# Host-side layouts for a streaming HGRN2 / forgetting-attention layer: inputs by feature, cached forget bias added on VectorE

## The chip, the cores and the metric

The kernel runs on one NeuronCore of one Trainium2 chip. The metric is device time in microseconds (us), the median of several runs; data that the host rearranges before the launch or after it is not in the time. TensorE (PE) multiplies and transposes, ScalarE (ACT) and VectorE (DVE) evict and compute elementwise, GpSimd (POOL) does small elementwise work and issues some DMAs, and SyncE (SP) issues the rest. 16 DMA engines move the data.

## The reference, cut to what matters

Two request groups go through one layer with the same weights: a prompt of 2048 tokens and 8 running streams of 16 tokens (the sample, 128 rows together). One projection feeds three mixers; forgetting attention of the sample reads 4096 cached rows of every stream:

```python
hq, hf, hi, hgate, fq, fk, fv, fgate, fflog, mq, mgate = _split_in(x @ w_in)
logf = jax.nn.log_sigmoid(fflog + b_forget)
# sample: keys, values, log forget values = cache followed by the new rows
D = jnp.cumsum(jnp.concatenate([past_logf, logf], axis=1), axis=1)
s = jnp.einsum('bthd,bshd->bhts', q, k) * (FX_DIM ** -0.5)
s = s + Dq[..., :, None] - Dk[..., None, :]      # the forget bias of a cached row is -Dk, up to a constant
p = jax.nn.softmax(jnp.where(mask, s, -jnp.inf), axis=-1)
o_fx = p @ v
o_mem = cross attention of mq into 256 memory rows (cached ones for the sample)
o_hg = gated linear recurrence of hq, hf, hi
y = layernorm(DN_ALPHA * x + concat(gated o_hg, o_fx, o_mem) @ w_out)
```

Besides y the outputs are the keys, values and log forget values of the new rows, the memory keys and values, and the recurrence states. All arrays are float32. x has 1024 features, w_in 3844 columns; the four forgetting heads have 64 features each.

## The kernel before, in words

TensorE contracts over the partitions, so both operands of a projection must have the features on the partitions. Tokens arrive with tokens on the partitions. `load_xT` (L248) loads half a tile (128 tokens x 512 features, buffer `xr`, three of them), lets TensorE transpose it in four pieces into a PSUM bank `tr`, and splits it into a rounded part (`xh`, ACT) and a rest (`xl`, DVE). Every projection is then three products per 128 features, 24 matmuls in all; the text calls these 24 matmuls one project. `load_w` and `split_next` (L275, L287) do the same split with the weights, 256 columns (a chunk) at a time.

Two passes go over 14 chunks of columns. Pass 1 has prompt tiles 0 to 7 and the sample tile in three groups of 384 tokens, pass 2 has tiles 8 to 15 (groups of 384, 384 and 256 tokens). An "f" chunk takes two projects per group, each with up to 384 columns moving; a "t" chunk (fox values, HGRN values) takes one project per tile with 256 or 260 columns moving. Pass 1 is 93 projects and pass 2 is 90. Results are evicted by ACT and DVE and spilled to DRAM from buffers that are double. `ev_fk` (L369) also transposes the new keys back to token rows for the output `p_fox_k`, as `mem_keys` (L481) does for the memory keys.

Other streams are woven between the matmuls of the projects. `tick` (L1103) is called four times per project, advances a clock by 0.25 and lets each stream take as many steps as an interpolation table (`PROG`, L1098) asks for. The first stream is the sample's: attention into the cached memory (4 pairs of streams), then forgetting attention over the caches (4 pairs), then its recurrence. It takes `DECODE_STEPS + 9` steps between clock 28 and clock 159; the row maxima of the prompt's forgetting attention run between 112 and 161. Steps only fix the traced order; a planner then orders the instructions of each engine by this priority and by simulated readiness.

`decode` (L619) handles one pair of streams. First the scores: for each of 8 chunks of 512 cached rows (1 for the memory) and each of the two streams it fetches a key tile (`kv`, 128 rows on partitions, 4 x 256 elements, 512 KB), transposes its eight 128x128 blocks on TensorE in two groups of four, ACT copies each group to a buffer `kT`, and each of these four copies is a step. As the fifth step it computes the scores in PSUM (`ds`, one bank): a matmul of the forget bias rows against a 0/1 matrix (`indr` x `rb`; the bias is held as a rounded part and a rest, 16 rows), then 4 x 2 matmuls of `kT` against the queries on quarters of the array; DVE takes the row maximum (L645) and ACT copies the scores to `S` (L646). After a softmax step come the values: two steps per chunk, four transposes of `S`, a DVE copy, and 32 small matmuls against two value tiles (`dv`). Key and value tiles share a ring of three buffers (`B_KV`), fetched one ahead on the SP queue; `rb` has two buffers and is fetched on the POOL queue.

After the passes, from about 975 us, come the prompt's mixers and the output projection, which work on spilled data.

Of the kernel before, what the change touches and what calls it, by code (L numbers as in the profile page):

```python
# [20 lines left out]
B_KV, B_KT, B_PJ, B_TR, B_DS = [3, 4, 3, 2, 1]  # L21
# [10 lines left out]

_CONST_PARTS = [
    ("ident", 128), ("lm", 192), ("bm", 128), ("ones", 128),
    ("tri", 128), ("cst", 128), ("cts", 128), ("sufblk", 128), ("nmask", 224), ("ind", 128), ("ind4", 128),
# [11 lines left out]
def _constants():  # L47
# [29 lines left out]
    r = np.arange(16)  # L77
    rowbh = (p // 64) * 4 + (p // 16) % 4
    put("ind", (r[:, None] % 8) == rowbh[None])
# [8 lines left out]
def kernel(  # L88
# [4 lines left out]
    w_mem_kv, w_out, ln_g, ln_b, consts,  # L93
# [8 lines left out]
    mem = mem_prompt[0]  # L102
    st_in = state_hgrn[0]
    ck = cache_fox_k[0].rearrange("b s h d -> b s (h d)")
    cv = cache_fox_v[0].rearrange("b s h d -> b s (h d)")
    clf = cache_fox_logf[0]
    cmk = cache_mem_k[0].rearrange("b s h d -> b s (h d)")
    cmv = cache_mem_v[0].rearrange("b s h d -> b s (h d)")
    win = w_in[0]
    wkv = w_mem_kv[0]  # L110
# [3 lines left out]
    o_pk = p_fox_k[0, 0].rearrange("t h d -> t (h d)")  # L114
    o_pv = p_fox_v[0, 0].rearrange("t h d -> t (h d)")
    o_pl = p_fox_logf[0, 0]
    o_mk = p_mem_k[0, 0].rearrange("t h d -> t (h d)")
    o_mv = p_mem_v[0, 0].rearrange("t h d -> t (h d)")
    o_sk = s_fox_k[0].rearrange("b t h d -> (b t) (h d)")
# [27 lines left out]
    s_r = dr.tile([4, 2, 8, 4096], F32, name="s_r")  # L147
# [17 lines left out]
    indr = ca.tile([16, 128], F32R, name="indr")  # L165
# [10 lines left out]
    def setup():  # L176
# [6 lines left out]
        DVE.tensor_copy(indr, const("ind")[0:16])  # L183
# [50 lines left out]
    # ------------------------------------------------------------------ input projections  # L234
# [13 lines left out]
    def load_xT(hi, lo, off, src):  # L248
        for half in range(2):
            xr = sg.tile([128, 512], F32, name="xr", bufs=B_XR)  # L250
            SP.dma_start(xr, src[:, half * 512 : half * 512 + 512])
            pt = ptr()
            for j in range(4):
                PE.transpose(pt[:, j, :], xr[:, j * 128 : j * 128 + 128], ident)
            d = slice(half * 4, half * 4 + 4)
            ACT.copy(hi[:, d, off : off + 128], pt)
            DVE.tensor_tensor(out=lo[:, d, off : off + 128], in0=pt, in1=hi[:, d, off : off + 128].bitcast(F32),
                              op=ALU.subtract)
# [4 lines left out]
    def fetch_ahead():  # L263
        while at["fetched"] < min(len(jobs), at["split"] + B_WR):
            job = jobs[at["fetched"]]
            job["raw"] = wp.tile([128, KW, 260], F32, name="wraw", bufs=B_WR)
            o, k = 0, job["k"]
            for s in job["srcs"]:
                n = s.shape[1]
                SP.dma_start(job["raw"][:, :, o : o + n],  # L270
                             s[128 * k : 128 * (k + KW)].rearrange("(k p) c -> p k c", p=128))
                o += n
            at["fetched"] += 1
# [13 lines left out]
    def load_w(srcs, w, pool=None):  # L287
        hi = (pool or wp).tile([128, 8, 260], F32R, name="whi")
        lo = (pool or wp).tile([128, 8, 260], F32R, name="wlo")
        for k in range(0, 8, KW):  # L290
            jobs.append(dict(srcs=srcs, w=w, hi=hi, lo=lo, k=k))
# [77 lines left out]
    def ev_fk(ps, mt, g):  # L369
# [13 lines left out]
        npt = g["np"] // 128  # L383
        SP.dma_start(o_pk[g["p0"] : g["p0"] + g["np"], c].rearrange("(j p) c -> p j c", p=128), kt[:, 0:npt, :])
        if g["s"]:
            SP.dma_start(o_sk[:, c], kt[:, npt, :])
            POOL.tensor_copy(ksT[:, mt, :], kf[:, n - 128 : n])
# [29 lines left out]
    def wc(a, n=256):  # L417
        return [win[:, a : a + n]]

    CHUNKS = [  # L420
        ("t", [win[:, 2560:2816], win[:, 3072:3076]], 260, ev_fv),
# [15 lines left out]
    def load_group(xg, gi, tiles, first=None):  # L437
# [3 lines left out]
        for j, t in enumerate(tiles):  # L441
            load_xT(hi, lo, j * 128, xs if t == "s" else xp[t * 128 : t * 128 + 128])
# [31 lines left out]
    # memory keys and values of the prompt group, and the forget bias of the cached rows  # L474
# [6 lines left out]
    def mem_keys(wk):  # L481
        for mt in range(2):
            ps = feature_major(wk, mt, mh, ml, 256)
            ACT.copy(mkT[:, mt, :], ps)
            pt = ptr()
            for j in range(2):
                PE.transpose(pt[:, j, :], mkT[:, mt, j * 128 : j * 128 + 128], ident)
            kt = ev("r", 256, bufs=1).rearrange("p (j c) -> p j c", c=128)
            ACT.copy(kt, pt[:, 0:2, :])
            SP.dma_start(o_mk[:, mt * 128 : mt * 128 + 128].rearrange("(j p) c -> p j c", p=128), kt)  # L490
# [22 lines left out]
    def cache_bias():  # L513
# [5 lines left out]
        a = oth[:, 0:256, :]  # L519
        POOL.tensor_tensor(out=a, in0=cur[:, 1:257, :], in1=off.unsqueeze(1).to_broadcast([128, 256, 4]), op=ALU.add)  # L520
        rh = mpool.tile([128, 4, 256], F32R, name="cbh")
        rl = mpool.tile([128, 4, 256], F32R, name="cbl")
        av = a.rearrange("p i h -> p h i")
        pin(ACT.copy(rh, av))
        DVE.tensor_tensor(out=rl, in0=av, in1=rh.bitcast(F32), op=ALU.subtract)
        for i, t in enumerate((rh, rl)):
            for bb in range(8):
                r0 = 4 * (bb % 2)
                SP.dma_start(s_r[bb // 2, i, r0 : r0 + 4].rearrange("h (k i) -> k h i", i=256),
                             t[16 * bb : 16 * bb + 16].bitcast(F32))  # L530
# [6 lines left out]
    def after1(i):  # L537
        if i == 0:
            for j in range(2):
                load_xT(mh, ml, j * 128, mem[j * 128 : j * 128 + 128])  # L540
            cache_scan()
        elif i == 1:
            mem_w.append(load_w([wkv[:, 0:256]], 256, pool=mpool))
        elif i == 2:
            split_next(mem_w[0][2])
            mem_keys(mem_w[0])
            mem_w.append(load_w([wkv[:, 256:512]], 256, pool=mpool))
# [5 lines left out]
    # ------------------------------------------------------------------ sample attention over the caches  # L553
# [36 lines left out]
    def cache_tile(src, r0, n):  # L590
        def f():
            t = dpool.tile([128, 4, 256], F32, name="kv", tag="kv", bufs=B_KV)
            SP.dma_start(t[:, 0 : n // 128, :], src[r0 : r0 + n].rearrange("(j p) c -> p j c", p=128))
# [11 lines left out]
    for kc, vc, rows, n in ((cmk, cmv, 256, 256), (ck, cv, 4096, 512)):  # L605
        for p in range(4):
            for src in (kc, vc):
                for c in range(0, rows, n):
                    for bb in range(2):
                        cache_issues.append(cache_tile(src[2 * p + bb], c, n))  # L610
# [8 lines left out]
    def decode(p, qbd, ns, new, dst, s_gate):  # L619
        nch = ns * 128 // 512 if new else 1  # L620
        cw = 512 if new else 256
        st = cw // 128
# [3 lines left out]
        for c in range(nch):  # L626
            kt = []
            for bb in range(2):
                kr = next_cache()
                for hp in range(2):  # L630
                    pt = ptr()
# [704 lines left out]
```

## Time and profile before

| what | value |
|---|---|
| median of 3 runs | 1681.04 us (1679.24 to 1684.19) |
| profiled execution, span from first to last instruction | 1683.6 us |
| PE busy | 1606.2 us, 95% |
| DVE, ACT, POOL busy | 47%, 35%, 11% |
| DMA, share of the 16 engines; bytes moved | 53%; 248.10 MB |
| mean granted TensorE clock | 0.989 |

The profiled execution's own time is its span, 1683.6 us, which lies inside the spread of the three runs. "Busy" for PE joins overlapping matmuls, and their ends are modelled, so the cost of an inserted instruction is best read from the start times of the matmuls around it.

### The profile page before, as it was taken

The page shows a single profiled execution, that of the slowest core. Times are in us where ns is not written, and L with a number is a line of the kernel's source. Part 1 is how long each engine was busy: PE and PEld are TensorE (multiplying, and loading weights), DVE is VectorE, ACT ScalarE, POOL GpSimd, SP SyncE. Part 2 cuts the span into 40 slices and gives each one's busy share as a digit, 9 for nine tenths or more (in the row PEclk, how much of TensorE's full clock was granted, in tenths as well). Part 3 has the DMA queues.
Part 4 walks back from the last instruction along what each step waited for, and adds up shares of the span by engine and source line. Part 5 has one row for each costly group of instructions (what it writes and reads, how often), then busy time and mean ns, then how long its engine had stood idle before and what let it go on. Part 6 is the DMA issues. An engine that isn't in the chain of part 4 may idle for free.

```text
span 1683.6 us, 31554 instructions
## 1 busy us (share of the span) xinstructions
PE 1606.2 (95%) x12885; PEld 1268.0 (75%) x12885; DVE 793.2 (47%) x1600; ACT 586.0 (35%) x1279; POOL 184.7 (11%) x251
## 2 busy tenths in 40 slices
PE   7999999999999998999999999989999999999998
PEld 7999998888887787788777886746566565567776
DVE  4222222221233234455446523267757666667785
ACT  4323333323342433023321033355434333343341
POOL 0610000000000220001001022321010110100000
PEclk9999999999999999999999999999999999999999
DMA  7555464466467764766556477596444343322321
GB/s 233 180 137 157 123 183 144 145 200 188 147 180 246 197 187 120 230 166 169 157 150 195 116 168 140 121 215 182 112 98 110 89 101 95 105 85 63 108 95 57
DMA packets 273984, 248.10 MB, mean 147 GB/s; under 512 B 44846, under 2 KB 251630, under 8 KB 273840
## 3 DMA queue, kind: packets, MB, share of 16 engines
q1 hardware_dynamic: 219408, 209.52, 41.4%
q0 software_dynamic: 54432, 36.56, 11.0%
q8 instruction: 102, 1.67, 0.4%
q14 instruction: 42, 0.34, 0.1%
HBM read 192.28 MB, written 53.64 MB: 146 GB/s over the span
## 4 chain that ended last, share of the span: by engine, by line
PE 74%; DMA 16%; DVE 4%; ACT 2%; issue 1%; SPq 1%; POOL 0%; DVEq 0%; ACTq 0%
PE pj L132 34%; PE o L132 10%; PE h L132 6%; PE pv L132 5%; PE f L132 5%; DMA kv<-in_cache_fox_v_dram 4%; PE tr L633 3%; PE ds L132 3%; DMA wraw<-in_w_in_dram 3%; PE dv L132 2%; DMA fP<-s_fg 2%; DMA hF<-s_f 2%; DMA xr<-in_x_prompt_dram 2%; PE tr L132 1%; PE L L132 1%
## 5 line engine op out<-in xcount | busy, mean ns | idle before, releaser
L132 PE MATMUL pj<-xh,whi 128*128 128x384 f32 (+1 forms) x1056 | 366.2, 347 | 6.1 <-DVE fmx L960 4.8
L132 PE MATMUL pj<-xl,whi 128*128 128x384 f32 (+1 forms) x1056 | 349.5, 331 | 0.0
L132 PE MATMUL pj<-xh,wlo 128*128 128x384 f32 (+1 forms) x1056 | 349.3, 331 | 0.0
L132 PEld LDWEIGHTS pj<-xh,whi 128*128 128x128 f32 x1056 | 200.9, 190 | 27.1 <-issue 16.7
L132 PEld LDWEIGHTS pj<-xl,whi 128*128 128x128 f32 x1056 | 200.8, 190 | 7.7 <-issue 3.7
L132 PEld LDWEIGHTS pj<-xh,wlo 128*128 128x128 f32 x1056 | 199.8, 189 | 2.0 <-issue 1.8
L960 DVE TENSOR_REDUCE fmx<-pj 128x1 f32<-128x512 f32 (+3 forms) x160 | 96.9, 609 | 84.7 <-PE pj L132 83.7
L1046 ACT ACTIVATE fP<-f 128x512 f32<-128x512 f32 (+3 forms) x144 | 73.1, 527 | 150.1 <-PE f L132 142.4
L635 ACT COPY kT<-tr 128x512 f32<-128x512 f32 (+1 forms) x144 | 81.0, 563 | 125.5 <-PE tr L633 125.0
L132 PE MATMUL pj<-whi,xh 128*128 128x256 f32 (+1 forms) x408 | 121.3, 298 | 0.0
L281 DVE TENSOR_TENSOR wlo<-wraw,whi 128x1024 fp32r<-128x1024 f32 (+1 forms) x60 | 76.4, 1273 | 95.3 <-ACT whi L280 94.7
L326 ACT ACTIVATE e<-pj 128x384 f32<-128x384 f32 (+1 forms) x96 | 45.4, 474 | 207.2 <-PE pj L132 196.9
L132 PE MATMUL pj<-wlo,xh 128*128 128x256 f32 (+1 forms) x408 | 117.5, 288 | 0.0
L1019 DVE TENSOR_TENSOR facc<-facc,fP 128x512 f32<-128x512 f32 (+3 forms) x144 | 83.8, 597 | 71.3 <-ACT fP L1046 71.0
L132 PE MATMUL pj<-whi,xl 128*128 128x256 f32 (+1 forms) x408 | 117.0, 287 | 0.0
L132 PE MATMUL pv<-fP,fV 128*64 128x512 f32 (+3 forms) x288 | 103.5, 551 | 4.2 <-ACT fP L1046 3.9
L132 PE MATMUL f<-fq,fk 68*128 68x512 f32 (+5 forms) x320 | 100.7, 406 | 1.9 <-DMA fk<-s_kk 0.9
L132 PEld LDWEIGHTS f<-fq,fk 68*128 68x128 f32 (+1 forms) x320 | 54.1, 193 | 55.3 <-issue 45.9
L132 PEld LDWEIGHTS pj<-whi,xh 128*128 128x128 f32 x408 | 78.0, 191 | 10.0 <-issue 9.1
L633 PE MATMUL tr<-cb,kv 128*128 128x128 f32 x544 | 83.5, 274 | 1.4 <-DMA kv<-in_cache_fox_k_dram 1.2
L280 ACT CAST whi<-wraw 128x1024 fp32r<-128x1024 f32 (+1 forms) x60 | 62.8, 1047 | 60.3 <-DMA wraw<-in_w_in_dram 55.6
L1032 POOL DMA_DIRECT2D fk<-s_kk x40 | 40.0, 999 | 399.9 <-PE f L132 399.9
(328 smaller groups left out, 2786.7 us busy)
## 6 DMA issues: line engine op xcount, KB each, us to landing
kv<-in_cache_fox_k_dram SPq DMA_DIRECT2D x64, 512.0 KB, 5.0
kv<-in_cache_fox_v_dram SPq DMA_DIRECT2D x64, 512.0 KB, 4.9
wraw<-in_w_in_dram SPq DMA_DIRECT2D x56, 512.0 KB, 5.4
fk<-s_kk POOLq DMA_DIRECT2D x40, 256.0 KB, 4.8
xr<-in_x_prompt_dram SPq DMA_DIRECT2D x32, 256.0 KB, 4.1
y<-in_x_prompt_dram SPq DMA_DIRECT2D x16, 512.0 KB, 3.3
out_dram<-y SPq DMA_DIRECT2D x16, 512.0 KB, 2.6
fk1m<-s_kk POOLq DMA_DIRECT2D x20, 272.0 KB, 7.8
```

The lines of the kernel that those rows point to most:

```text
L132: PE.matmul(out, lhsT=lhsT, rhs=rhs, start=start, stop=stop)
L280: pin(ACT.copy(hi[:, r, :w], raw[:, :, :w]))
L281: pin(DVE.tensor_tensor(out=lo[:, r, :w], in0=raw[:, :, :w], in1=hi[:, r, :w].bitcast(F32), op=ALU.subtract))
L326: ACT.activation(e, ps, AF.Sigmoid)
L633: PE.transpose(pt[:, j, :], kr[:, j, hp * 128 : hp * 128 + 128], ident)
L635: ACT.copy(k2[:, 0:cw], pt[:, 0:st, :].rearrange("p j c -> p (j c)"))
L960: DVE.tensor_reduce(out=mx[:, hh, tt, c : c + 1], in_=ps, axis=AX.X, op=ALU.max)
L1019: DVE.tensor_tensor(out=acc[hh][:, t0:], in0=acc[hh][:, t0:], in1=PT[hh][:, t0:], op=ALU.add)
L1032: POOL.dma_start(k1, s_kk[64:132, hs, cs])
L1046: ACT.activation(pT[:, t0:], ps[:, t0:], AF.Exp)
```

## The change

The host now writes the inputs into DRAM in the order in which tiles read them, and turns outputs back afterwards.

- x and the prompt's memory tokens lie by feature; `load_xT` loads [128 features, 4, 128 tokens] and splits it at once, with no transpose.
- weights lie so that each partition reads one contiguous row; a fetch is one DMA.
- cached keys lie as [stream, 2, 128 features, rows]; a key tile is read as [128, 2, 512] and goes straight into the score matmuls. The transposes, the ACT copies and the `kT` buffers are gone; the ring `B_KV` has five buffers, fetched three ahead. Cached values lie so that each partition reads one contiguous row of 4 KB.
- the forget bias is kept in float32 (not as two rounded rows), 8 rows per pair of streams; it is fetched on the SP queue as a [128, 512] tile, each row repeated 16 times, and one DVE instruction adds it to the scores, writes `S` and takes the maximum. The bias matmul, and for the forgetting attention the ACT copy to `S`, are gone.
- new keys and memory keys are written by feature, without transposes; the 16 small stores of the log forget values are one; states are read and written by partition.
- a score chunk is one step, not five: `DECODE_STEPS` goes from 277 to 133, inside the same table `PROG`.

```diff
-B_KV, B_KT, B_PJ, B_TR, B_DS = [3, 4, 3, 2, 1]
+B_KV, B_PJ, B_TR, B_DS = [5, 3, 2, 1]
...
     def load_xT(hi, lo, off, src):
         for half in range(2):
-            xr = sg.tile([128, 512], F32, name="xr", bufs=B_XR)
-            SP.dma_start(xr, src[:, half * 512 : half * 512 + 512])
-            pt = ptr()
-            for j in range(4):
-                PE.transpose(pt[:, j, :], xr[:, j * 128 : j * 128 + 128], ident)
             d = slice(half * 4, half * 4 + 4)
-            ACT.copy(hi[:, d, off : off + 128], pt)
+            xr = sg.tile([128, 4, 128], F32, name="xr", bufs=B_XR)
+            SP.dma_start(xr, src[:, d, :])
+            ACT.copy(hi[:, d, off : off + 128], xr)
...
-        pt = ptr()
-        nt = n // 128
-        for j in range(nt):
-            PE.transpose(pt[:, j, :], kf[:, j * 128 : j * 128 + 128], ident)
-        kt = ev("r", n, bufs=1).rearrange("p (j c) -> p j c", c=128)
-        ACT.copy(kt, pt[:, 0:nt, :])
...
+        SP.dma_start(p_fox_k[c, g["p0"] : g["p0"] + g["np"]], kf[:, 0 : g["np"]])
...
+    def key_tile(src, b, r0, n):
+        def f():
+            t = dpool.tile([128, 2, 512], F32, name="kv", tag="kv", bufs=B_KV)
+            SP.dma_start(t[:, :, 0:n], src[b, :, :, r0 : r0 + n].rearrange("c p s -> p c s"))
+            return t
...
     def bias_tile(p, c):
         def f():
-            t = dpool.tile([16, 512], F32R, name="rb", bufs=2)
-            POOL.dma_start(t, s_r[p].rearrange("i r s -> (i r) s")[:, c * 512 : c * 512 + 512])
+            t = dpool.tile([128, 512], F32, name="rb", bufs=2)
+            SP.dma_start(t, s_r[p, :, c * 512 : c * 512 + 512].unsqueeze(1).to_broadcast([8, 16, 512]))
...
         for c in range(nch):
-            kt = []
-            for bb in range(2):
-                kr = next_cache()
-                for hp in range(2):
-                    pt = ptr()
-                    for j in range(st):
-                        PE.transpose(pt[:, j, :], kr[:, j, hp * 128 : hp * 128 + 128], ident)
-                    k2 = dpool.tile([128, 512], F32, name="kT", tag="kT", bufs=B_KT)
-                    ACT.copy(k2[:, 0:cw], pt[:, 0:st, :].rearrange("p j c -> p (j c)"))
-                    kt.append(k2)
-                    yield
+            kt = [next_cache(), next_cache()]
...
-            if new:
-                mm(ps, indr, bias_get(8 * p + c), start=True, stop=False)
...
-            DVE.tensor_reduce(out=mx[:, c : c + 1], in_=ps, axis=AX.X, op=ALU.max)
-            ACT.copy(S[:, c * cw : c * cw + cw], ps)
+            if new:
+                DVE.tensor_tensor_reduce(out=S[:, c * cw : c * cw + cw], in0=ps, in1=bias_get(8 * p + c), scale=1.0,
+                                         scalar=NEG, op0=ALU.add, op1=ALU.max, accum_out=mx[:, c : c + 1])
+            else:
+                DVE.tensor_reduce(out=mx[:, c : c + 1], in_=ps, axis=AX.X, op=ALU.max)
+                ACT.copy(S[:, c * cw : c * cw + cw], ps)
...
-    DECODE_STEPS = 1 + 4 * (5 + 1 + 2 + 1) + 4 * (8 * 5 + 1 + 9 * 2 + 1)
+    DECODE_STEPS = 1 + 4 * (1 + 1 + 2 + 1) + 4 * (8 + 1 + 9 * 2 + 1)
```

## Rows read from the trace of the kernel before

**Rows 1.** The page's head, its part 1 (busy time and share of the span) and its chain that ended last, by engine.

```profile
span 1683.6 us, 31554 instructions
...
PE 1606.2 (95%) x12885; PEld 1268.0 (75%) x12885; DVE 793.2 (47%) x1600; ACT 586.0 (35%) x1279; POOL 184.7 (11%) x251
...
PE 74%; DMA 16%; DVE 4%; ACT 2%; issue 1%; SPq 1%; POOL 0%; DVEq 0%; ACTq 0%
```

**Rows 2.** Busy time by stretch: the first 50 us, the rest of the two passes, the mixers. Columns: stretch and its length, busy us of each engine, granted clock, DMA share, GB/s.

```profile
0.00:50.00 50.00, 41.52 (x310) 39.59 (x310) 22.63 (x49) 20.59 (x36) 5.23 (x10) 1.00 0.78 240
50.00:975.00 925.00, 884.21 (x6556) 774.63 (x6555) 329.07 (x617) 295.08 (x503) 92.01 (x133) 0.99 0.58 167
975.00:1683.60 708.60, 680.46 (x6023) 453.76 (x6021) 441.50 (x935) 270.36 (x741) 87.43 (x109) 0.99 0.45 115
```

**Rows 3.** Waits of PE between 0 and 975 us: who waited for whom, us in total, times, longest.

```profile
PE tr L254 <- DMA xr<-in_x_prompt_dram: 11.2, 8, 4.9
PE dv L132 <- DMA kv<-in_cache_fox_v_dram: 10.1, 13, 2.0
...
PE ds L132 <- ACT kT L635: 4.1, 3, 3.1
...
PE tr L633 <- DMA kv<-in_cache_fox_k_dram: 1.2, 2, 0.8
```

**Rows 4.** Groups of instructions with their shapes: the PE work that the diff takes out (busy us and mean ns of one; matmuls of one group overlap).

```profile
L633 PE MATMUL tr<-cb,kv 128*128 128x128 f32 x544 | 83.5, 274 | 1.4 <-DMA kv<-in_cache_fox_k_dram 1.2
...
L254 PE MATMUL tr<-cb,xr 128*128 128x128 f32 x152 | 25.5, 297 | 13.3 <-DMA xr<-in_x_prompt_dram 11.2 <-DMA xr<-in_mem_prompt_dram 1.0 <-DVE xl L257 0.8
...
L132 PE MATMUL ds<-rb,indr 16*128 16x512 f32 x32 | 15.8, 493 | 0.0
...
L379 PE MATMUL tr<-cb,e 128*128 128x128 f32 x34 | 6.1, 284 | 0.6 <-ACT e L372 0.6
```

**Rows 5.** PE in order of time inside a project while a key tile is transposed (start us, us, engine, line, operation).

```profile
284.30 0.34 PE L132 MATMUL pj<-xl,whi 128*128 128x384 f32 x1
284.48 0.34 PE L132 MATMUL pj<-xh,wlo 128*128 128x384 f32 x1
284.65 0.60 PE L633 MATMUL tr<-cb,kv 128*128 128x128 f32 x4
285.00 0.42 PE L132 MATMUL pj<-xh,whi 128*128 128x384 f32 x1
285.26 0.33 PE L132 MATMUL pj<-xl,whi 128*128 128x384 f32 x1
```

**Rows 6.** The same around the scores of one chunk of cached rows.

```profile
293.61 0.34 PE L132 MATMUL pj<-xh,wlo 128*128 128x384 f32 x1
293.87 0.49 PE L132 MATMUL ds<-rb,indr 16*128 16x512 f32 x1
294.30 1.06 PE L132 MATMUL ds<-kT,qbd 128*32 128x512 f32 x8
295.29 0.44 PE L132 MATMUL pj<-xh,whi 128*128 128x384 f32 x1
295.57 0.34 PE L132 MATMUL pj<-xl,whi 128*128 128x384 f32 x1
```

**Rows 7.** The same at the value matmuls of two chunks that follow each other.

```profile
363.38 1.07 PE L132 MATMUL dv<-kv,pT 128*32 128x128 f32 x28 [0.54 <-DMA kv<-in_cache_fox_v_dram]
...
368.33 1.07 PE L132 MATMUL dv<-kv,pT 128*32 128x128 f32 x28
```

**Rows 8.** Busy time by stretch, columns as in rows 2: a stretch of key chunks, of value chunks, the key chunks beside `ev_fk` in pass 2, and a stretch near the end.

```profile
240.00:340.00 100.00, 100.00 (x634) 88.11 (x633) 20.82 (x33) 36.50 (x63) 3.90 (x8) 1.00 0.48 148
340.00:400.00 60.00, 58.75 (x614) 48.88 (x614) 12.10 (x18) 15.99 (x26) 0.49 (x1) 1.00 0.71 221
...
560.00:600.00 40.00, 38.15 (x235) 30.43 (x234) 8.02 (x12) 16.24 (x32) 10.92 (x19) 1.00 0.90 257
...
1600.00:1650.00 50.00, 49.06 (x524) 36.92 (x519) 39.39 (x83) 19.46 (x65) 0.00 (x0) 1.00 0.24 80
```

**Rows 9.** DMA issues of a kind: queue, count, KB each, median us from issue to landing.

```profile
kv<-in_cache_fox_k_dram SPq DMA_DIRECT2D x64, 512.0 KB, 5.0
kv<-in_cache_fox_v_dram SPq DMA_DIRECT2D x64, 512.0 KB, 4.9
...
y<-in_x_prompt_dram SPq DMA_DIRECT2D x16, 512.0 KB, 3.3
...
fq<-s_qq POOLq DMA_DIRECT2D x8, 512.0 KB, 8.7
...
rb<-s_r POOLq DMA_DIRECT2D x32, 32.0 KB, 3.2
```

**Rows 10.** Groups of instructions on DVE and ACT, as in rows 4: the maximum and the copy of the scores, a two-operand DVE instruction that reads PSUM, and the split of x.

```profile
L257 DVE TENSOR_TENSOR xl<-tr,xh 128x512 fp32r<-128x512 f32 x34 | 23.4, 692 | 27.2 <-ACT xh L256 27.1
L1250 DVE SCALAR_TENSOR_TENSOR y<-y,o 128x512 f32<-128x512 f32 x34 | 23.2, 684 | 17.3 <-PE o L132 17.3
...
L645 DVE TENSOR_REDUCE mx<-ds 128x1 f32<-128x512 f32 x32 | 22.1, 692 | 84.3 <-PE ds L132 84.3
...
L256 ACT CAST xh<-tr 128x512 fp32r<-128x512 f32 x34 | 19.9, 588 | 33.4 <-PE tr L254 29.3 <-PE pj L132 3.7
L646 ACT COPY S<-ds 128x512 f32<-128x512 f32 x32 | 18.8, 587 | 72.2 <-DVE mx L645 72.2
```

More of the change, by code (lines that the diff above doesn't have):

```diff
@@ L146 @@
     s_ms = dr.tile([2, 8, 128, 128], F32, name="s_ms")
-    s_r = dr.tile([4, 2, 8, 4096], F32, name="s_r")
+    s_r = dr.tile([4, 8, 4096], F32, name="s_r")
     cb = cp.tile([128, _CONST_B], F32, name="cb")
@@ L164 @@
     nmb = ca.tile([128, 224], BF16, name="nmb")
-    indr = ca.tile([16, 128], F32R, name="indr")
     ind4r = ca.tile([8, 128], F32R, name="ind4r")
@@ L249, in load_xT @@
         for half in range(2):
-            xr = sg.tile([128, 512], F32, name="xr", bufs=B_XR)
-            SP.dma_start(xr, src[:, half * 512 : half * 512 + 512])
-            pt = ptr()
-            for j in range(4):
-                PE.transpose(pt[:, j, :], xr[:, j * 128 : j * 128 + 128], ident)
             d = slice(half * 4, half * 4 + 4)
-            ACT.copy(hi[:, d, off : off + 128], pt)
-            DVE.tensor_tensor(out=lo[:, d, off : off + 128], in0=pt, in1=hi[:, d, off : off + 128].bitcast(F32),
+            xr = sg.tile([128, 4, 128], F32, name="xr", bufs=B_XR)
+            SP.dma_start(xr, src[:, d, :])
+            ACT.copy(hi[:, d, off : off + 128], xr)
+            DVE.tensor_tensor(out=lo[:, d, off : off + 128], in0=xr, in1=hi[:, d, off : off + 128].bitcast(F32),
                               op=ALU.subtract)
@@ L266, in fetch_ahead @@
             job["raw"] = wp.tile([128, KW, 260], F32, name="wraw", bufs=B_WR)
[L267 to L272, printed above, removed]
+            k, w = job["k"], job["w"]
+            SP.dma_start(job["raw"][:, :, 0:w], job["src"][:, k : k + KW, :])
             at["fetched"] += 1
@@ L484, in mem_keys @@
             ACT.copy(mkT[:, mt, :], ps)
-            pt = ptr()
[L486 to L490, printed above, removed]
+            SP.dma_start(p_mem_k[mt * 128 : mt * 128 + 128], mkT[:, mt, :])
     def mem_values(wv):
@@ L518, in cache_bias @@
         pin(DVE.tensor_copy(off, pt[:, 0, 0:4]))
[L519 to L530, printed above, removed]
+        at = mpool.tile([128, 4, 256], F32, name="cbh")
+        POOL.tensor_tensor(out=at.rearrange("p h i -> p i h"), in0=cur[:, 1:257, :],
+                           in1=off.unsqueeze(1).to_broadcast([128, 256, 4]), op=ALU.add)
+        for bb in range(8):
+            SP.dma_start(s_r[bb // 2, 4 * (bb % 2) : 4 * (bb % 2) + 4].rearrange("h (k i) -> k h i", i=256),
+                         at[16 * bb : 16 * bb + 16])
     A1 = [[0, 1, 2], [3, 4, 5], [6, 7, "s"]]
@@ L604 @@
     cache_issues = []
-    for kc, vc, rows, n in ((cmk, cmv, 256, 256), (ck, cv, 4096, 512)):
+    for kc, vc, rows, n in ((cache_mem_k, cache_mem_v, 256, 256), (cache_fox_k, cache_fox_v, 4096, 512)):
         for p in range(4):
-            for src in (kc, vc):
-                for c in range(0, rows, n):
-                    for bb in range(2):
-                        cache_issues.append(cache_tile(src[2 * p + bb], c, n))
+            for c in range(0, rows, n):
+                cache_issues += [key_tile(kc, 2 * p + bb, c, n) for bb in range(2)]
+            for c in range(0, rows, n):
+                cache_issues += [value_tile(vc, 2 * p + bb, c // n, n) for bb in range(2)]
     cache_at = [0]
@@ L643, in decode @@
                     j = bb * 2 + hp
-                    mm(ps[32 * j : 32 * j + 32, :], qbd[:, 2 * p + bb, hp, :], kt[j][:, 0:cw], start=not new, stop=True)
-            DVE.tensor_reduce(out=mx[:, c : c + 1], in_=ps, axis=AX.X, op=ALU.max)
-            ACT.copy(S[:, c * cw : c * cw + cw], ps)
+                    mm(ps[32 * j : 32 * j + 32, :], qbd[:, 2 * p + bb, hp, :], kt[bb][:, hp, 0:cw])
+            if new:
[4 more added lines that the diff above has]
+                ACT.copy(S[:, c * cw : c * cw + cw], ps)
             yield
@@ L899, in prompt_forget_rows @@
         DVE.tensor_copy(lt[:, 32:64], lp[:, 36:68])
-        for i in range(16):
-            SP.dma_start(o_pl[128 * i : 128 * i + 128], lt[:, 4 * i : 4 * i + 4])
+        SP.dma_start(p_fox_logf, lt)
         pt = ptr()
@@ L1324 @@
     arrays, args = {}, []
-    for name in _INS + ["consts"]:
-        a = _constants() if name == "consts" else np.ascontiguousarray(inputs[name])
+    laid = _layouts(inputs)
+    for name in _INS:
+        if name not in laid:
+            args.append(None)
+            continue
+        a = laid[name]
         arrays[f"in_{name}_dram"] = a
         args.append(nc.dram_tensor(f"in_{name}_dram", a.shape, mybir.dt.from_np(a.dtype), kind="ExternalInput").ap())
-    for i, (shape, dtype) in enumerate(_OUTS):
-        dt = mybir.dt.from_np(np.dtype(dtype))
-        args.append(nc.dram_tensor(f"out_{i}_dram", shape, dt, kind="ExternalOutput").ap())
+    for i, shape in enumerate(_OUTS):
+        args.append(nc.dram_tensor(f"out_{i}_dram", shape, F32, kind="ExternalOutput").ap())
     with tile.TileContext(nc) as tc:
@@ L1334 @@
     r = _run(nc, [arrays], core_ids=[0])
-    return tuple(r.results[0][f"out_{i}_dram"] for i in range(len(_OUTS)))
+    return _results(r.results[0][f"out_{i}_dram"] for i in range(len(_OUTS)))
```

94 lines of the change are left out of this document (54 added, 40 removed), and 3 rows, old and new, of the table _OUTS.

## The prediction

> **What bounds the kernel now.** I read the page's busy shares and its chain first: PE is busy for 95% of the span and carries 74% of the chain that ended last [rows 1]. Busy time by stretch then shows where this can change. In the two passes PE is idle for 8.5 us of the first 50 and for 41 us of the next 925; the 708.6 us of the mixers hold no line of the diff [rows 2], so I leave them as they are. The waits of PE show what the idle time of the passes is made of: 11.2 us for x, 10.1 us for cached values, 4.1 us for the copies of transposed keys [rows 3]. So up to 975 us the kernel is a queue of PE instructions: time goes where PE instructions go, unless DMA becomes late. DMA is the only other resource near a limit. Its share is 0.48 at 148 GB/s among key chunks, 0.71 at 221 among value chunks, 0.90 at 257 where the keys stand beside `ev_fk` [rows 8]. Dividing rate by share gives 308, 311, 286 and, in a late stretch, 333 GB/s; I take 310 as what the 16 engines can move.
>
> **What leaves PE.** Prices are differences of start times, since matmuls overlap. Two neighbouring matmuls of a project start 0.18 us apart (284.30 and 284.48; 24 of them, at 0.175 us, are a project of 4.2 us). With four transposes between them the same two steps take 285.26 - 284.48 = 0.78 us, so a group of four costs 0.78 - 0.35 = 0.43 us [rows 5].
> - Cached keys: 544 transposes [rows 4], of which 512 are forgetting attention, 128 groups of four: 128 x 0.43 = 55 us. The other 32 are the memory's, 16 groups of two at an estimated 0.25 us: 4 us.
> - The bias matmul: the score matmuls start 294.30 - 293.87 = 0.43 us behind it [rows 6], 32 times: 14 us. The rest of a score chunk on PE is 295.57 - 293.61 - 0.35 - 0.43 = 1.18 us and stays.
> - New keys and memory keys: 34 transposes [rows 4] in 12 groups of three or two, and 4 more: about 5 us.
> - x: 152 transposes [rows 4], 38 groups. 16 are in pass 2 (6.9 us), 22 in the first 50 us (9.5 us). That first stretch runs at a DMA share of 0.78 [rows 2] and PE already waits for x [rows 3]; without its transposes it is a chain of loads into three buffers, each released only when DVE has made `xl` (0.59 + 0.69 us behind the landing, [rows 10]). I count 5 us there and 5 in pass 2: 10 us.
>
> Together 88 us.
>
> **Waits that go.** A value chunk took 368.33 - 363.38 = 4.95 us for 1.05 MB [rows 7] with a ring of three. With five buffers and two steps of 0.92 project each, a value chunk gets some 9 us, so the 10.1 us of waiting for values goes; the 4.1 and 1.2 us about transposed keys go with the transposes [rows 3]: 15 us. What is late next is the key tile.
>
> **What is added.** A score chunk is now one step. 142 steps (133 + 9) over 131 units of the clock make 0.92 project per step, so two key tiles (1.05 MB) and one bias tile (0.26 MB) are wanted per step. Where an "f" chunk runs beside it, PE needs 0.92 x 4.2 + 1.18 = 5.05 us for a step. Weights (1.05 MB per 6 projects) and spills (0.20 MB per project) add 0.34 MB: 1.65 MB, 5.33 us at 310 GB/s, 0.28 us late. By the clock the scores of the four pairs fall at projects 47, 73, 99 and 125, eight steps each:
> - pair 0, as above: 0.28 us.
> - pair 1 beside the "t" chunks at the end of pass 1, where a project has 256 columns (2.8 us): PE needs 3.8 us, 1.54 MB need 5.0: 1.2 us.
> - pair 2 beside `ev_fk`, which spills 0.59 MB per project: 2.02 MB need 6.5 us against 5.05: 1.45 us.
> - pair 3 beside the row maxima, which give PE more to do: nothing.
>
> 8 x (0.28 + 1.2 + 1.45) = 23 us that PE waits for keys. Below, this cost is bounded by the late stretch's 333 GB/s, where `y` tiles of 512 KB with 4 KB rows land in 3.3 us (13 us); above, by the slowest load of the same shape, `fq` on POOL, 512 KB as 2 KB rows out of a strided array, 8.7 us against 5.0 for a key tile now [rows 9]. Key tiles become 2 KB rows out of a strided array, but on SP, without the cast that `fq` has; I take the engines' rate as nearest, since `kv` on SP is the nearest row, and keep both ends.
>
> DVE's new instruction stands in no row. Its nearest are the maximum (692 ns) and a two-operand instruction that reads PSUM (684 ns); if it took both in turn it would be 1.4 us, about the 692 + 587 ns by which `ds` is held now [rows 10]. The next scores come 3.8 us later at the earliest, so it costs PE nothing; from 3.8 us on it would. It waits for the bias tile, and behind it on DVE stand the evictions and the splits of weights. Two bias buffers, one fetched ahead, give about a step; `rb` lands in 3.2 us now [rows 9], at 32 KB, and `pj` has three banks, two projects of slack: nothing. SP issues 32 bias loads more, while POOL loses them, and a bias load that waits for its buffer holds key loads and spills behind it; both are released by the same step, so I count nothing and leave it to the range. The copies that leave ACT, the smaller bias split, fewer weight DMAs and the stores of the log forget values are beside PE work: nothing either way. The key output is now read from the buffer that the sigmoids share, held some us longer: nothing, up to 5 us in the six `ev_fk` projects of each pass.
>
> **Sum.** 88 + 15 - 23 = 80 us. 1683.6 - 80 = 1603.6 for an execution like the profiled one, which is 2.6 us above the median; I forecast 1603.
>
> **A rule against it.** The bias load's outermost source dimension is 8. The Trainium skill, DMA: Bandwidth & Descriptors, section Why a DMA increments its semaphore by 16 and not by 1, says that a DMA uses the largest number of engines up to 16 that divides the outermost dimensions of both sides, here 8, the lowest-numbered ones. No row of this kernel shows a transfer on half the engines.
>
> **Rivals.**
> - *Half the engines carry the bias.* Then 0.26 MB counts double on the engines that end last: 0.26 / 310 GB/s = 0.85 us more per step, 27 us over 32 steps, less some 3 in pair 3, where PE has room: 1603 + 24 = 1627. For it: the new tile's first dimension is 8, repeated 16 times. Against: the other loads can fill the idle half, and the ring of five lets them run ahead. Chance 0.2.
> - *The keys are not late.* Larger rows (4 KB values and weights, 2 KB keys) may lift the rate enough: the 23 us are not paid and x gives its whole 16 us: 1603 - 23 - 6 = 1574. For it: 333 GB/s where 4 KB rows are moved [rows 8]. Against: 257 GB/s at 0.90 beside `ev_fk`. Chance 0.22.
> - *Slower: the strided key tile.* A key tile reads 2 KB out of each 16 KB row. At the price of `fq`, 8.7 us each, with three in flight, two tiles need 5.8 us: 24 us over 32 steps, still faster. It becomes slower than before from the point where a step is held by 88 + 15 = 103 us / 32 = 3.2 us beyond its 5.05: 8.3 us for two tiles, 12.4 us for one with three in flight. At 14 us for a tile a step is 9.3 us: 32 x 4.25 = 136 us, 1681 + 33 = 1714. For it: 8.7 us already without such a load beside it. Against: that load is on another queue and casts. Chance 0.05. The same skill page, section Latency and other measured facts, gives falling rates for rows 512 KiB or more apart; 16 KiB lies below its range, and no run here shows it.
> - *The transposes were free,* hidden in gaps of PE: 1681. Against: the start times of the matmuls around them move apart by 0.43 us [rows 5]. Chance 0.03.
>
> The rest, 0.5, is the forecast with its own errors (1588 to 1617).
>
> **How the numbers follow.** The range takes in both middle rivals with some margin for a planner that orders the new instructions otherwise: 1566 to 1648, which leaves out the two last rivals and about one in ten beyond. A measurement of this kernel can tell 0.3%, 5 us, from no change. Faster by more: the forecast and the first two rivals, and 0.01 of the third, at its low end: 0.93. Within: 0.03, the free transposes. Slower: 0.04, the rest of the third.
>
> **What would show it.** Right: PE's busy time some 85 to 90 us lower, all of it before about 900 us; neighbouring project matmuls 0.18 us apart with only `ds`, `dv` and `S` transposes between them; score chunks at about 1.2 us on PE; no wait for cached values; new waits of `ds` for key tiles, most in pairs 1 and 2; a DMA share of 0.9 or more in those stretches; the mixers still at about 709 us. Half the engines: long landings of `rb`, and key waits in pair 0 as well. Wrong: PE waits beside the key chunks above 50 us, landings of key tiles above 10 us, a granted clock well below 0.99 there, or a first 50 us that does not shrink while x is no later.

## The result, and the profile after

The changed kernel took 1605.22 us (median of four runs, 1597.58 to 1608.52) beside 1682.62 us for the kernel before in the same session: 0.9552 of its time, 95% interval 0.9509 to 0.9596. The prediction was 1603 us, within 1566 to 1648. That the two lie so close is in part luck: as the experiments show, about as much time was lost beside the key tiles as forecast, but half of it to the bias loads, which had been put at nothing.

First the profiled execution after: the page's head, busy times and chain by engine and by line, to be held against [rows 1].

```profile
span 1595.8 us, 29721 instructions
...
PE 1512.4 (95%) x12119; PEld 1183.6 (74%) x12119; DVE 794.4 (50%) x1630; ACT 481.7 (30%) x1088; POOL 168.7 (11%) x219
...
PE 71%; DMA 15%; DVE 6%; issue 4%; ACT 3%; SPq 1%; POOL 0%; DVEq 0%; ACTq 0%; POOLq 0%
PE pj L119 32%; PE o L119 11%; PE pv L119 6%; PE h L119 6%; PE f L119 6%; DMA wraw<-in_w_feat_dram 4%; DMA rb<-s_r 2%; PE ds L119 2%; PE dv L119 2%; DMA fP<-s_fg 2%; PE L L119 1%; PE tr L119 1%; DMA xr<-in_x_feat_dram 1%; PE h L1172 1%; DVE wlo L259 1%
```

PE's busy time fell by 93.8 us and the span by 87.8; PE's idle time grew by 6 us. `rb<-s_r`, the bias tile, now stands in the chain by itself. Busy time by stretch, columns as in [rows 2]: the first 50 us, the rest of the passes, the mixers (which now begin near 900 us).

```profile
0.00:50.00 50.00, 36.02 (x248) 34.25 (x249) 26.45 (x49) 21.54 (x38) 12.79 (x13) 1.00 0.76 238
50.00:900.00 850.00, 809.38 (x5953) 710.82 (x5952) 329.96 (x651) 193.33 (x315) 74.25 (x106) 0.99 0.63 194
900.00:1595.80 695.80, 667.04 (x5923) 438.52 (x5921) 438.02 (x931) 266.80 (x736) 81.61 (x102) 0.98 0.45 112
```

The first load of `fP` of the mixers is issued at 921.8 us instead of 1010.3: 88.5 us earlier, so the whole gain lies in the passes. The waits of PE between 0 and 900 us (waiter, releaser, us in total, times, longest) answer to [rows 3].

```profile
PE pj L119 <- DMA fq1m<-s_qq: 13.4, 5, 5.6
PE pj L119 <- DVE fmx L917: 12.2, 8, 4.1
PE pj L119 <- ACT whi L258: 8.7, 1, 8.7
PE ds L119 <- DVE mx L600: 5.9, 6, 1.6
...
PE ds L119 <- DMA kv<-in_cache_fox_k_dram: 1.1, 1, 1.1
```

The waits for cached values and for transposed keys are gone. But PE waits 1.1 us for key tiles, where 23 us were forecast. What is late stands on DVE. One tile's view, `rb` in the changed kernel: its instructions (ns min/median/max, first and last start) and what the engine that uses it waited for (us, times).

```profile
L567 SPq DMA_DIRECT2D rb<-s_r x32: 594/604/717, 139.3 to 679.7; - x32
L600 DVE CUSTOM_DVE_ANT_0 S<-ds,rb x32: 678/691/693, 232.4 to 689.3; 128x512 f32<-128x512 f32 x32
...
  DMA rb<-s_r: 53.6, 14
```

DVE's new instruction takes 691 ns, as long as the old maximum alone. It stood 53.6 us, in 14 of 32 cases, before a bias tile that had not landed. In order of time beside the "t" chunk of pass 1 (start us, us, engine, line, operation, and in brackets the idle time before it):

```profile
355.15 0.61 SPq L567 DMA_DIRECT2D rb<-s_r  x1
355.60 0.69 DVE L600 CUSTOM_DVE_ANT_0 S<-ds,rb 128x512 f32<-128x512 f32 x1
...
356.34 1.07 PE L119 MATMUL ds<-kv,qbd 128*32 128x512 f32 x8 [0.25 <-DVE mx L600]
...
361.26 0.69 DVE L600 CUSTOM_DVE_ANT_0 S<-ds,rb 128x512 f32<-128x512 f32 x1 [4.97 <-DMA rb<-s_r]
...
362.02 1.36 PE L119 MATMUL ds<-kv,qbd 128*32 128x512 f32 x8 [1.59 <-DVE mx L600]
```

The load issued at 355.15 releases DVE at 361.26, 6.1 us later. This is the shortest of the 14 cases: they take 6.1 to 13.7 us from issue to the start on DVE, 9.3 in the middle. Scores were ready and idle in the only `ds` bank meanwhile; PE gets it back at 362.02, and a step takes 362.02 - 356.34 = 5.7 us, where PE alone needed 3.8 by the prediction's prices.

### The profile page after: what moved, and what is told of

Its sections match the earlier page's. It is cut to its first block, busy times and chain, and to the rows that moved or that the text cites. A ratio compares the mean times of both kernels' runs of the same rounds, so it can differ in the third digit from the quotient of the medians.

```text
span 1595.8 us, 29721 instructions
## 1 busy us (share of the span) xinstructions
PE 1512.4 (95%) x12119; PEld 1183.6 (74%) x12119; DVE 794.4 (50%) x1630; ACT 481.7 (30%) x1088; POOL 168.7 (11%) x219
## 4 chain that ended last, share of the span: by engine, by line
PE 71%; DMA 15%; DVE 6%; issue 4%; ACT 3%; SPq 1%; POOL 0%; DVEq 0%; ACTq 0%; POOLq 0%
PE pj L119 32%; PE o L119 11%; PE pv L119 6%; PE h L119 6%; PE f L119 6%; DMA wraw<-in_w_feat_dram 4%; DMA rb<-s_r 2%; PE ds L119 2%; PE dv L119 2%; DMA fP<-s_fg 2%; PE L L119 1%; PE tr L119 1%; DMA xr<-in_x_feat_dram 1%; PE h L1172 1%; DVE wlo L259 1%
## 5 line engine op out<-in xcount | busy, mean ns | idle before, releaser
L119 PE MATMUL pj<-xh,whi 128*128 128x384 f32 (+1 forms) x1056 | 360.9, 342 | 2.8 <-DVE fmx L917 2.7
L119 PE MATMUL pj<-fk1m,fq1m 66*128 66x512 f32 (+3 forms) x160 | 64.7, 406 | 23.4 <-DMA fq1m<-s_qq 13.4
L119 PEld LDWEIGHTS pj<-whi,xl 128*128 128x128 f32 x408 | 78.4, 192 | 4.9 <-DVE xl L239 4.0
```

What stands on the lines that cost most here:

```text
L119: PE.matmul(out, lhsT=lhsT, rhs=rhs, start=start, stop=stop)
```

## The experiments

Runs of one group shared a chip, on which the kernel before took 1687.54, 1690.80 or 1686.74 us; so ratios to it are compared. Theory A: the bias load, whose source has 8 stored rows, is carried by half of the DMA engines. Rivals: it is asked for too late; repeated reads of the same rows are slow; the keys are late all the same, by volume.

**The bias stored twice** (first group). Source of 16 rows, each to 8 partitions.

```diff
-    s_r = dr.tile([4, 8, 4096], F32, name="s_r")
+    s_r = dr.tile([4, 16, 4096], F32, name="s_r")
-            SP.dma_start(t, s_r[p, :, c * 512 : c * 512 + 512].unsqueeze(1).to_broadcast([8, 16, 512]))
+            SP.dma_start(t, s_r[p, :, c * 512 : c * 512 + 512].unsqueeze(1).to_broadcast([16, 8, 512]))
```

> The bias rows are stored twice in DRAM, so that a bias load has 16 rows repeated 8 times as its source instead of 8 rows repeated 16 times; the same 256 KB land in the same tile. Theory A (the load runs on half of the engines and is late for that): landings of the bias tile in the key chunks fall from 6 to 10 us to about 5, DVE's 53.6 us of waiting for it fall below 20 us, and the time falls by 10 to 25 us, to 1580 to 1595 us. Theory B (all engines are full there, and the load stands behind two key tiles): DVE's wait stays within 45 to 60 us and the time at 1600 to 1610 us. Theory C (two buffers are too few, so each load starts only when the score chunk two before has been read): as B.

1588.83 us, ratio 0.9409 (0.9368 to 0.9450): 0.0143 below the changed kernel's 0.9552, 24 us, with some 10 us on either side from the two intervals. DVE's wait for the bias fell less than expected, from 53.6 to 32.8 us; what DVE waited for in the view of `rb`:

```profile
  DMA rb<-s_r: 32.8, 9
```

Where DVE waited, a tile landed 5.1 to 12.4 us after its issue, 7.9 in the middle, and not at the expected 5.

**The bias loaded once per pair** (first group): `bias_tile(p, 0)` for all chunks of a pair, which leaves out the bias of the other seven.

> The bias tile is loaded once per pair of streams (4 loads, not 32), and every score chunk adds the bias of the first chunk: the bias of the other chunks is left out. An upper bound of what the bias loads cost by any theory. If the key stage is bound by what the engines move, 1.05 instead of 1.31 MB a step take the key stage off the limit: the waits of PE for the scores' bank (13.2 us) and most of the waits of DVE (53.6 us) go, and the time falls by 15 to 25 us, to 1580 to 1590 us. If bias loads hide beside PE, the time stays at 1600 to 1610 us.

1583.97 us, ratio 0.9367 (0.9318 to 0.9416). With 28 of 32 bias loads away this is the gain without what they cost: 0.0633 x 1682.6 = 107 us. It is 26 to 31 us below the changed kernel's two ratios (the second one is below). PE and its weight loads waited 1.1 us in all for key tiles here: without the bias they are hardly late.

**Two steps per score chunk** (first group): a `yield` behind each chunk's maximum, `DECODE_STEPS` 165.

> A score chunk takes two steps of the clock, not one (DECODE_STEPS 165), so the same loads are wanted at half the pace and the value chunks come somewhat closer together (a step is 131/174 = 0.75 project). If the key chunks are bound by what the engines move per step (theories A and B): PE's waits in the key chunks go, 1585 to 1595 us. By theory C too. If PE is not held by them: 1600 to 1610 us.

1602.88 us, ratio 0.9476 (0.9422 to 0.9530), DVE's wait 26.1 us. The wait halved, the time did not follow as far; its interval meets that of the changed kernel. By its ratio the run lies at the edge of the first expectation (0.9476 x 1682.6 = 1594 us), by its own microseconds in the second, so it decides nothing.

**The bias back on TensorE** (first group): rounded part and rest, `indr` matmul, 32 KB loads on POOL, maximum and ACT copy as before; keys still by feature.

> The bias goes back to TensorE: two rounded rows of bias, the matmul against the 0/1 matrix, the maximum on DVE and the copy on ACT, and the 32 KB load on POOL; keys stay by feature. PE pays 32 x 0.43 = 14 us again; the 256 KB loads go. By the prediction's terms: 1605 + 14 - 15 to 25 = 1594 to 1604 us. If the bias loads cost nothing: 1619 us.

1589.06 us, ratio 0.9415 (0.9371 to 0.9460). This is the change without its fourth part, the bias on VectorE, and it is faster than the whole change. It also lies below the 1594 to 1604 us that were expected: the loads that go cost more than was counted, or the matmul less.

**Loads alone** (second group). Nothing is computed; 32 loads of each shape are issued back to back.

> This kernel leaves out the whole computation: it issues five phases of 32 loads each, up to six in flight, on SyncE's queue: the bias tile as the changed kernel reads it (8 stored rows, each to 16 partitions), the bias tile from 16 stored rows (each to 8 partitions), the key tile by feature, the value tile by rows of 4 KB, and a key tile by rows of 1 KB. Theory A (the bias load of 8 rows is carried by half of the DMA engines): the first phase shows a DMA share of 0.5 or less and about half the rate of the second, which has a share above 0.9. If repeated reads of the same stored row are what makes the bias load slow, both bias phases show the same share and nearly the same rate, below the rate of the value tiles. If the key tile by feature costs more than one by rows, its phase is longer than that of the 1 KB rows; my prediction said that only its volume counts: the three phases of 512 KB tiles should then lie within 10% of each other, at 32 x 0.524 MB over some 1.6 us each, near 300 GB/s and about 55 us each.

Busy time by stretch (length, busy us of DVE and POOL, granted clock, DMA share, GB/s): bias from 8 rows, bias from 16 rows (two stretches), keys by feature, values, 1 KB rows.

```profile
14.00:50.00 36.00, 3.69 (x24) 0.00 (x0) 1.00 0.53 177
64.00:71.00 7.00, 1.07 (x7) 0.00 (x0) 1.00 1.01 300
71.00:88.00 17.00, 2.77 (x18) 0.00 (x0) 1.00 1.03 265
95.00:130.00 35.00, 3.85 (x26) 0.00 (x0) 1.00 1.05 387
134.00:170.00 36.00, 4.21 (x28) 0.00 (x0) 1.00 1.03 410
176.00:215.00 39.00, 4.00 (x26) 0.00 (x0) 1.00 1.10 348
```

With six loads in flight and nothing else running, the bias load keeps 0.53 of the engines' time busy; from 16 rows it keeps all of it. The Trainium skill, DMA: Bandwidth & Descriptors, section Why a DMA increments its semaphore by 16 and not by 1, has the rule: the largest count up to 16 that divides the outermost dimensions. For 8 rows that is 8 engines, and 0.53 agrees. The key tile by feature, 387 GB/s, is faster than one by rows of 1 KB, 348. Two expectations missed: the bias from 8 rows moves at 0.6 to 0.7 of the rate from 16, not at half, and the three kinds of 512 KB tile differ by 18%, not 10, all above 300 GB/s. Even on all engines the bias is the slowest shape. Whether its repeated reads make it so is not shown: its tile is also half as large as the others, and from 8 rows, with twice as many repeats, rate over share is higher (177 / 0.53 = 334) than from 16 (300 / 1.01 = 297, 265 / 1.03 = 257).

**Keys transposed again** (second group): the run with the bias back on TensorE, with the transposes, `kT`, the old steps and a ring of three back as well. Key tiles come by token rows, four rows (4 KB) to a partition in one piece, where the kernel before read pieces of 1 KB.

> The run with the bias added on TensorE (keys still by feature) stood at 0.9415 of the kernel before. Here the cached keys come by token rows again and are transposed on TensorE, so of the change only the x, memory, weight and new-key parts are left. My prediction priced the cached and memory keys' transposes and their waits at 55 + 4 + about 15 us: the ratio should rise by about 0.040 to 0.045, to about 0.984 (some 1655 us where before is 1682). If the transposes had been nearly free (hidden beside other work), the ratio stays within 0.950.

1667.54 us, ratio 0.9852 (0.9823 to 0.9881): 0.0437 above the run with the bias on TensorE, 74 us, with some 9 us on either side from the two intervals. Waits of PE in this run up to 900 us: those that the change had removed are back.

```profile
PE dv L122 <- DMA kv<-in_cache_fox_v_dram: 11.8, 11, 2.4
...
PE ds L122 <- ACT kT L612: 3.3, 2, 2.4
```

**x transposed again** (second group).

```diff
-            ACT.copy(hi[:, d, off : off + 128], xr)
+            pt = ptr()
+            for j in range(4):
+                PE.transpose(pt[:, j, :], xr[:, j, :], ident)
+            ACT.copy(hi[:, d, off : off + 128], pt)
```

> Only the tokens of x and of the memory prompt come by rows again and are transposed on TensorE; all else is as in the changed kernel (0.9552). My prediction gave this part 10 of the 16.4 us that these transposes took: ratio 0.961. If the transposes of x lie beside loads that the start waits for anyway, the ratio stays at 0.955 to 0.957; if all count, 0.965.

1618.31 us, ratio 0.9572 (0.9550 to 0.9595): 0.002 to 0.005 above the changed kernel's two ratios (below), 3 to 9 us, which the intervals don't tell from none. The trace is sharper. Groups of PE instructions in the first 50 us of this run, with their count:

```profile
L119 PE MATMUL pj<-whi,xh 128*128 128x260 f32 x72 | 21.2, 297 | 0.0
...
L240 PE MATMUL tr<-cb,xr 128*128 128x128 f32 x84 | 15.0, 310 | 8.7 <-DMA xr<-in_x_feat_dram 8.4
L119 PE MATMUL pj<-xh,whi 128*128 128x384 f32 x3 | 1.2, 393 | 0.0
```

That is 225 project matmuls (72 and 3 of each of three kinds); without the transposes the changed kernel has 248 by then, all of its PE instructions in the first row of its stretches above. 23 more at 0.175 us are 4.0 us. Over the whole passes the traces show more than the ratios: the first load of `fP` is issued at 940.0 us here and at 921.8 and 927.6 in the two profiled executions of the changed kernel, 12 to 18 us earlier. So what x is worth lies between 3 and 18 us, and 10 was forecast.

**The bias stored four times** (second group), 32 rows, each to 4 partitions.

> The forget bias is stored four times, so that a bias tile is read from 32 stored rows, each to 4 partitions. Theory A (with 8 rows half of the engines carry the load, with 16 rows all of them): nothing more to gain, the ratio is that of 16 rows, 0.941 within 0.004. Theory B (the same stored row is read over and over by many packets, and that is slow): fewer repeats gain again, the ratio falls to 0.937 or less, near that of the run without the later bias loads, and VectorE's wait for the bias tile falls from 32.8 us to below 15.

1596.20 us, ratio 0.9435 (0.9413 to 0.9457), DVE's wait 13.6 us. In time this is theory A, no gain over two copies; in the wait it is what theory B said. So the rest of DVE's wait, 32.8 us with two copies, cost TensorE nothing that the time shows.

**The changed kernel again** (third group).

> The changed kernel itself, unaltered, on the chip on which the next three run, so that they can be compared with it directly: ratio to the kernel before 0.955 within 0.005, as before.

1605.12 us, ratio 0.9521 (0.9483 to 0.9560).

**Three bias buffers** (third group), two fetched ahead, the load as in the change.

> Three bias buffers instead of two, so that two bias tiles are fetched ahead; the load itself stays as it is, from 8 stored rows. If the bias tile is late because it is asked for too late (a step's notice against a landing of some 5 us), this alone gains most of what storing the rows twice gained: ratio 0.941 to 0.945. If it is late because it is carried by half of the engines, which then have 0.53 us-engines too much in each step, fetching it earlier only moves the wait to other tiles of the same queue: 0.950 or more.

1599.74 us, ratio 0.9490 (0.9447 to 0.9532): 5 us, inside the intervals, and between the two expectations. The tile view of `ds` shows why: what its engines, matmuls and weight loads together, waited for (us, times).

```profile
  DMA kv<-in_cache_fox_k_dram: 14.7, 14
...
  DVE mx L600: 1.8, 3
```

No DVE instruction waits for a bias tile that has not landed, waits for the `ds` bank to be freed by the maximum come to 1.8 us instead of 13.2 and 14.5 in the two executions of the changed kernel, and the key tiles are late in 14 cases instead of 6 (4.2 and 7.3 us there). The wait moved, as the rival expectation said, and with the bias on all engines (next run) the keys are late in 7 cases, 9.5 us: this speaks for a shortage on the half of the engines that carries the bias.

**Both: the bias stored twice, three buffers** (third group).

> The bias stored twice and three bias buffers together. The run that loads the bias once per pair (0.9367) is the bound of what the bias loads can still give. If the rest of VectorE's wait for the bias (32.8 us with the rows stored twice) holds TensorE, this gains up to 0.004: 0.937. If TensorE has slack enough at that wait, no change: 0.941 within 0.003.

1589.81 us, ratio 0.9428 (0.9389 to 0.9468). The view of `rb` in this run:

```profile
L602 DVE CUSTOM_DVE_ANT_0 S<-ds,rb x32: 683/692/693, 231.7 to 677.6; 128x512 f32<-128x512 f32 x32
its engine sat idle before it (us, times) until:
  PE ds L119: 61.9, 26
who waited for it (us, times):
busy tenths in 40 slices 0000001000000000100000000000000000000000
DMA to landing us min/median/max: 3.4/7.0/8.2
```

Nobody waits for the bias any more, and the time is that of two buffers: once all engines carry it, its notice is enough. On this chip the step from the changed kernel is 1605.12 - 1589.81 = 15 us; from the first group it was 24. So half the engines cost 15 to 24 us by the medians, each with some 9 us on either side. In the profiled executions the first load of `fP` comes 6 to 16 us earlier with the bias stored twice (912.1 and 915.7 us against 921.8 and 927.6).

**Rows of 1 KB for values and weights** (third group): both are laid out by rows as before and read in 1 KB pieces.

> The cached values and the weights of the projections come in rows of 1 KB again instead of 4 and 2 KB; all else is as in the changed kernel. My prediction named no gain for these. With the keys by token rows, the whole key part and the bias undone, 25 us of gain were left, where I had priced the transposes of x and of the new keys at 15. If the longer rows are worth the difference, the ratio rises by 0.005 to 0.010 over the changed kernel on this chip; if the rows' length does not matter while DMA is hidden, it stays within 0.003.

1603.80 us, ratio 0.9531 (0.9480 to 0.9581): no gain of the longer rows is seen beside 0.9521, but the two intervals leave room for some 10 us, and the keys' rows were not changed here.

## Why the prediction was right, and where it was not

**The cached keys** (55 + 4 us of transposes and 15 of waits): 74 forecast, 74 measured, with some 9 us on either side, between the two runs that differ in them, their ring and their steps. PE's busy time between these two differs by 1587.7 - 1514.3 = 73.4 us, more than the 59 that start times gave, and the waits were worth less than counted, since PE's idle time differs by 10. So the sum is right and its split is not settled. The price by start times holds where it can be tried: in the kernel before, from the first to the last maximum of the scores in pair 0 (243.1 to 334.7 us), all matmuls at the prediction's prices come to 91.2 of 91.7 us.

**The score chunk**: 1.18 us on PE forecast. In the changed kernel's PE in order of time,

```profile
246.03 0.34 PE L119 MATMUL pj<-xh,wlo 128*128 128x384 f32 x1
246.30 1.06 PE L119 MATMUL ds<-kv,qbd 128*32 128x512 f32 x8
247.29 0.44 PE L119 MATMUL pj<-xh,whi 128*128 128x384 f32 x1
247.58 0.33 PE L119 MATMUL pj<-xl,whi 128*128 128x384 f32 x1
```

247.58 - 246.03 - 0.35 = 1.20 us. This holds for the chunks that PE does at once; 9 of 32 it does in pieces (below).

**x**: 5 us in the first stretch forecast, 4 seen. The reason was only half right: PE's largest wait there is now 8.7 us for `whi`, not for x. It is one wait, before the first matmul of all: the first weights have to land (ACT starts their split at 7.6 us) and be split.

**The bias matmul** (14 us): not confirmed. The run with the matmul (0.9415) stands 0.0048, 8 us, above the one with hardly any bias loads, inside the intervals, and level with those where VectorE adds the bias and all engines carry it (0.9409, 0.9428, 0.9435). Within the intervals, some 10 us on either side, the eight times larger loads give back what the matmul costs: this part of the change is worth nothing that the runs can tell when done well, and costs 15 to 24 us as done.

**The term that failed: "8 x (0.28 + 1.2 + 1.45) = 23 us that PE waits for keys".** (Its lower bound, 13 us at 333 GB/s, comes to 15 by its own volumes.) In the changed kernel PE waits 1.1 us for key tiles. The rate of 310 GB/s is not what failed. Loads alone are faster in the new shapes, 387 GB/s for the key tile and 410 for the values against 348 for rows of 1 KB, but under load this does not show: among the first key chunks and beside `ev_fk`, 275 / 0.86 = 320 and 287 / 0.91 = 315 (columns as in [rows 8]).

```profile
230.00:280.00 50.00, 50.00 (x303) 40.74 (x302) 14.60 (x33) 13.88 (x18) 0.00 (x0) 1.00 0.86 275
480.00:540.00 60.00, 56.50 (x310) 41.18 (x302) 15.89 (x50) 16.70 (x27) 9.45 (x16) 1.00 0.91 287
```

What failed is what the term said the time is lost to. The changed kernel from the first to the last start of DVE's new instruction in pairs 0, 1 and 2, seven of eight steps each:

```profile
232.40:269.50 37.10, 37.10 (x221) 29.46 (x220) 10.24 (x24) 5.24 (x9) 0.00 (x0) 1.00 0.95 299
349.90:386.70 36.80, 32.62 (x225) 22.11 (x225) 6.00 (x15) 3.56 (x8) 0.00 (x0) 1.00 0.88 278
477.80:529.70 51.90, 49.35 (x270) 34.57 (x269) 14.98 (x48) 10.94 (x22) 8.40 (x14) 1.00 0.90 281
```

In pair 1 PE starts 225 matmuls, of which 56 are the seven score chunks of 1.18 us and the others 7 projects of 2.8 us: 28 of 36.8 us, so 9 us are lost. In the same way nothing is lost in pair 0 and 11 us in pair 2. That is the size that was forecast (2, 8 and 10 us for seven steps). But only 4.2 and 2.6 us of it are idle time of PE, and it is not the keys' volume alone: with the bias stored twice 6 and 9 us are lost in pairs 1 and 2, with most bias loads gone 1 and 8. What is left without the bias lies for the most part in score chunks that PE does in pieces, with project matmuls between. The changed kernel does 9 of its 32 chunks so (3 in the kernel before), as here in pair 1:

```profile
378.18 1.05 PE L119 MATMUL ds<-kv,qbd 128*32 128x512 f32 x4
379.16 0.39 PE L119 MATMUL pj<-whi,xh 128*128 128x256 f32 x1
...
379.71 1.05 PE L119 MATMUL ds<-kv,qbd 128*32 128x512 f32 x4
380.70 0.39 PE L119 MATMUL pj<-whi,xh 128*128 128x256 f32 x1
```

Four of the eight matmuls take 379.16 - 378.18 = 0.98 us, as long as all eight above (247.29 - 246.30 = 0.99), so such a chunk costs about 1 us more, as busy time that no row of waits shows. That the planner orders them so because it expects the second key tile late is likely, but not shown.

**The step that failed with it: "Two bias buffers, one fetched ahead, give about a step ... nothing".** It borrowed the landing of a 32 KB tile (3.2 us) for one of 256 KB, which on half the engines, behind the key tiles, took 6.1 to 13.7 us where DVE waited for it. The rival *Half the engines carry the bias* had the mechanism and priced it at 24 us (measured: 15 to 24), but stood on top of a loss beside the keys that is in good part its own: 1603 + 24. *The keys are not late*, 1574, was right that PE hardly waits for them, and wrong about the rate, which rose little under load; with all engines on the bias the kernel stands at 1589 to 1596, with most bias loads gone at 1584. So the stretches beside the keys lost about what was forecast, half of it to another cause, and that the sum met the time is to this extent luck. The strided key tile at the price of `fq` did not come: alone it lost 6% of the rate of the value tile, 387 against 410.

**What stays open.** The run with keys and bias undone is still 0.0148, 25 us, faster than the kernel before; x and the new keys were priced at 15 of it. The other 10 us, of which the interval covers about half, were not split. Row lengths are not excluded: the last run shortened those of values and weights alone, in a ring of five, and the run with the keys undone reads its keys in longer pieces than the kernel before. Its profiled execution issues the first load of `fP` at 994.1 us against 1010.3, only 16 us earlier.

## What to carry to other kernels

A time lost beside late loads need not stand as a wait: add up the matmuls of a stretch at their start-to-start prices and hold the sum against its length, for a matmul group in pieces counts as busy. A rate of a shape measured alone is a bound, not the rate under load: here 387 GB/s alone, 275 to 287 in the kernel. When a broadcast load from DRAM grows, look at its outermost dimension before its bytes: a DMA share near 0.5 under a full queue is the sign, and storing the source twice was the cure here (1589.81 us, against 1605.12 for the change and 1686.74 for the kernel before). A wait that vanishes with one more buffer while another grows points to a shortage of the resource behind both, more than of notice.

## What the runs showed of the hardware

Loads of the same length of piece, 2 KB, differed by a third: 387 GB/s for the key tile, where every piece is another stored row, against 265 to 300 for the bias, where 8 partitions read the same one, both with all engines busy; the bias tile is also half as large. Eight score matmuls on four quarters of the array took 0.99 us from start to start, the four of one stream, on two quarters, 0.98. And DVE adds two 128x512 operands, one of them in PSUM, and takes the row maximum with it in 691 ns, plus 83 ns to read the accumulator: no longer than the maximum alone.
